# Delta rule pipeline: products of a chunk over two PSUM banks, both products with the state issued first, and a spacing of its own for each chain

## The chip, the cores and the metric

The kernel runs on one core of one Trainium2 chip. The metric is the device time of one execution in microseconds, the median of the runs shown.

## The reference

Two model blocks follow each other on 512 tokens of width 1024. The change lies in the second, in the gated delta rule, which has 8 heads of width 128. What the reference computes for each chunk of a head (it uses chunks of 64 tokens; the kernel uses 4 chunks of 128, which gives the same result):

```python
t_inv = triangular_solve(eye + lmat, eye)        # lmat: strictly lower, from k k^T, decay, beta
u = t_inv @ v_beta
w = t_inv @ (k_beta * exp(gc))
def step(state, xs):
    q_c, k_c, u_c, w_c, a_c, gl = xs
    v_new = u_c - w_c @ state
    o_c = q_c @ state + a_c @ v_new
    state = state * gl + k_c.T @ v_new
    return state, o_c
```

Around it stand a projection of the input (q, k, v and a gate z per head), a causal convolution with SiLU, an RMS norm of o, the gate, and after all heads two more projections.

## The kernel before

All large products are split into two parts of fp32r each (hi and lo), so a product takes three matmuls per 128 rows of depth: whi with h2h, whi with h2l, wlo with h2h. ScalarE makes whi from a weight tile (`wraw`), GpSimd makes wlo (a subtraction of 128x1024 elements, line 359).

The delta stage works in ten slots, t = 0 to 9. In each slot a main generator (`project` of head t for t < 8, `gates` for t = 8 and 9) issues 32 units of three 512-column matmuls into the tag "mm"; here they are called units 0 to 31. After each unit `weave` lets side generators take a step, each at its own start and spacing counted in units:

- `pairs` of head t-1: score products (ta<-kq, gives NU and Aq on VectorE), the transposes of v, then 15 steps of a small solve on VectorE alone (row, dt, dh), which end in dc and Dk.
- `double` of head t-2, eight steps that build the inverse D of 128x128 from 32x32 blocks. Its products are, in order: N with Dk; PX with dc; NU with Dt (32x32 blocks); dc with P1; transposes of D; NU with Dt6; P16 with D. Between two of them VectorE or ScalarE makes the next operand (PX is one of VectorE's).
- `states` of head t-2, chained behind `double`: for each chunk c the products with the state (S with kq, twice), with D (gives vn, on ScalarE), and of vn with kd and with Aq. VectorE makes Wc and the next S, ScalarE and VectorE make the output O. A last step is a reciprocal square root of 4 columns (rs_v, rs_i, rs_j, rs_t, rs_y) and the scaling of O.
- `outputs` of head t-3: four transposes of O and the gate.
- `keys` of head t: norms of q and k, transposes.

TensorE runs in the order in which the generators issue (`chained(True)`, line 1737). The other engines' orders are made by a scheduler when the kernel is built. All products of a chunk but one go to four quarters of one PSUM tile `pa`; the one with kd goes to `pb`. Both have the tag "sm", which has two buffers of one bank each. The tag "tb" of `double` has one buffer. The three lines of `states` that the prediction speaks of most are 1693 to 1696:

```python
K.mm(pa[:, 0:128], kq[:, 0, c], S, start=True, stop=True)
Wc = dp.tile([128, 128], F32, name="Wc", tag="Wc", bufs=2)
nc.vector.scalar_tensor_tensor(Wc, pa[:, 0:128], egc[:, 1, h, c:c + 1], V[:, c], op0=OP.mult, op1=OP.add)
K.mm(pa[:, 128:256], kq[:, 1, c], S, start=True, stop=True)
```

After the last slot the output of head 7 is transposed and gated (line 1750), the stage's pool is closed, and ya is split into yah and yal for the next projection.

Of the kernel before, what the change touches and what calls it, by code (L numbers as in the profile page):

```python
# [11 lines left out]
AF = mybir.ActivationFunctionType  # L12
OP = mybir.AluOpType
# [14 lines left out]

def weave(main, sides):

    sides = [[g, a, d] for g, a, d in sides]
    for u, _ in enumerate(main):
        for q in sides:
            while q[0] is not None and q[1] <= u:
                if next(q[0], sides) is sides:
                    q[0] = None
                q[1] += q[2]
    for q in sides:
        for _ in q[0] or ():
            pass  # L40


def view(ap, off, dims):
# [196 lines left out]
class Core:  # L240
# [36 lines left out]
    chain = None  # L277
# [541 lines left out]
def body(tc, I, out, es):  # L819
# [413 lines left out]
    with ExitStack() as es2:  # L1233
        K.new_sp(es2, 416)
        hp = es2.enter_context(tc.tile_pool(name="hp2", bufs=1))
        nr = ffn(1, x, LAT, (mod['l1'],), lambda: None, hp, nr)
    block2(K, tc, I, out, x[0], mod['b2'], amod, nr)
    K.close_x()


def block2(K, tc, I, out, x, mod, amod, nr):
    nc, ones, ident = K.nc, K.ones, K.ident
    SEG = ((0, 512),)
    with ExitStack() as es:
# [21 lines left out]
        def bc(v, n=128):  # L1266
            return v[:, :, None].to_broadcast([128, v.shape[1], n])
# [18 lines left out]
        t = [dp.tile([128, 4, 8], F32, name=f"g{k}") for k in range(6)]  # L1286
# [21 lines left out]
        esf, egl = eg[:, 0], eg[:, 1]  # L1308
# [49 lines left out]
        scale = 64 ** -0.5  # L1358
        with ExitStack() as es2:
# [14 lines left out]
            for pr in range(2):  # L1374
                ot, zs, st = [], [], []
                for g, d in enumerate(DIL):
# [7 lines left out]
                    q, k, v = qkv  # L1384
# [9 lines left out]
                    for hh in range(2):  # L1394
# [3 lines left out]
                        if g == 0:  # L1398
                            for b0 in (0, 2):
                                p = K.pt("ta")  # L1400
                                for b in (b0, b0 + 1):
                                    o = (b - b0) * 256
                                    k0 = max(b - 1, 0) * 128
                                    n = 256 if b else 128
                                    nc.tensor.matmul(p[:, o + 256 - n:o + 256], q[rows, b * 128:b * 128 + 128], k[rows, k0:k0 + n],
                                                     start=True, stop=True)
# [99 lines left out]
        def t512(name):  # L1506
            return dp.tile([128, 4, 128], F32, name=name, tag=name, bufs=DBS.get(name, 2))
# [4 lines left out]
        def s4(name):  # L1512
            return sp.tile([128, 4], F32, name=name, tag=name, bufs=4)

        def tr4c(src, tag):
            p = K.pt(tag)
            for c in range(4):
                K.tp(p[:, c * 128:c * 128 + 128], src(c), ident)
            return p
# [4 lines left out]
        def project(h, H_):  # L1524

            H_.kq = dp.tile([128, 2, 4, 128], F32, name="kq", tag="kq", bufs=3)
            H_.vc, H_.za = t512("vc"), t512("za").rearrange("p a b -> p (a b)")
            dst = (H_.kq[:, 1].rearrange("p a b -> p (a b)"), H_.kq[:, 0].rearrange("p a b -> p (a b)"),
                   H_.vc.rearrange("p a b -> p (a b)"))
            for k in range(4):  # L1530
                p = K.pt("mm")
                yield from K.gemm_units(next(W), H, p)
                if k < 3:
                    conv(p, 8 * k + h, dst[k])
                else:
                    nc.scalar.activation(H_.za, p, AF.Silu)
                yield
# [143 lines left out]
        def states(h, H_):  # L1681

            kq, kd, V, D, Aq, bk = H_.kq, H_.kd, H_.V, H_.D, H_.Aq, H_.bk
            O = H_.O = t512("O")
            so = H_.so = s4("so")
            junk2 = dp.tile([128, 128], F32, name="junk2", tag="junk2", bufs=1)
            S = None
            for c in range(4):
                pa = K.pt("sm")
                if S is None:  # L1690
                    Wc = V[:, c]
                else:
                    K.mm(pa[:, 0:128], kq[:, 0, c], S, start=True, stop=True)
                    Wc = dp.tile([128, 128], F32, name="Wc", tag="Wc", bufs=2)
                    nc.vector.scalar_tensor_tensor(Wc, pa[:, 0:128], egc[:, 1, h, c:c + 1], V[:, c], op0=OP.mult, op1=OP.add)
                    K.mm(pa[:, 128:256], kq[:, 1, c], S, start=True, stop=True)
                    nc.scalar.activation(O[:, c], pa[:, 128:256], AF.Copy, scale=egc[:, 0, h, c:c + 1])
                    yield
                K.mm(pa[:, 256:384], D[:, c], Wc, start=True, stop=True)
                vn = dp.tile([128, 128], F32, name="vn", tag="vn", bufs=2)  # L1700
                nc.scalar.activation(vn, pa[:, 256:384], AF.Copy, scale=bk[:, c:c + 1])
                yield
                if c < 3:
                    pb = K.pt("sm")
                    K.mm(pb[:, :128], kd[:, c], vn, start=True, stop=True)
                    Sn = dp.tile([128, 128], F32, name="S", tag="S", bufs=2)
                    if S is None:
                        nc.vector.tensor_copy(Sn, pb[:, :128])
                    else:
                        nc.vector.scalar_tensor_tensor(Sn, S, egl[:, c, h:h + 1], pb[:, :128], op0=OP.mult, op1=OP.add)  # L1710
                K.mm(pa[:, 384:512], Aq[:, c], vn, start=True, stop=True)
                if S is None:
                    nc.vector.tensor_copy(O[:, c], pa[:, 384:512])
                else:
                    nc.vector.tensor_add(O[:, c], O[:, c], pa[:, 384:512])
                nc.scalar.activation(junk2, O[:, c], AF.Square, accum_out=so[:, c:c + 1])
                if c < 3:
                    S = Sn
                yield
            nc.vector.tensor_tensor(so, so, H_.rq2, op=OP.mult)  # L1720
            r = K.rsqrt(so, 4, 1.0 / 128, EPS)
            nc.vector.tensor_tensor(r, r, H_.rq, op=OP.mult)
            nc.vector.tensor_tensor(O, O, bc(r), op=OP.mult)

        def outputs(h, H_):
            p = tr4c(lambda c: H_.O[:, c], "sm")
            nc.vector.scalar_tensor_tensor(ya[:, h], p, K.s('dnorm'), H_.za, op0=OP.mult, op1=OP.mult)
            yield

        def gates(j0):  # L1730
            for j in range(j0, j0 + 4):
                p = K.pt("mm")
                yield from K.gemm_units(next(W), H, p)
                nc.scalar.activation(sga[:, j], p, AF.Sigmoid)
                yield

        K.chained(True)
        hs = [Head() for _ in range(8)]
        for t in range(10):
            sides = []  # L1740
            if 0 <= t - 1 < 8:
                sides.append((pairs(t - 1, hs[t - 1]), 1, 1.5))
            if 0 <= t - 2 < 8:
                sides.append((chain(double(t - 2, hs[t - 2]), states(t - 2, hs[t - 2])), 2, 1.6))
            if 0 <= t - 3 < 8:
                sides.append((outputs(t - 3, hs[t - 3]), 8, 1))
            if t < 8:
                sides.append((keys(t, hs[t]), 18, 6))
            weave(project(t, hs[t]) if t < 8 else gates(4 * t - 32), sides)
        weave((), [(outputs(7, hs[7]), 0, 1)])  # L1750
        K.chained(False)
        dp_es.close()
        with ExitStack() as es2:
# [45 lines left out]
```

## Time and profile before

| | us |
|---|---|
| runs shown | 2565.75, 2567.43, 2574.22 (median 2567.43) |
| profiled execution | 2574.59 |
| its span from the first to the last instruction | 2572.8 |
| of it the delta stage, from its first gemm matmul to the first matmul with yah | 2081.7 to 2467.8, 386 |
| mean granted TensorE clock | 0.975 of full speed |

The profiled execution is one execution. Its stretches are compared with each other below by their place in it; times of four digits before the point are microseconds from the start of its span. In the views, PE is TensorE, PEld its weight loads, DVE VectorE, ACT ScalarE and POOL GpSimd. A row by stretch has its bounds, its length, the busy time of PE, PEld, DVE, ACT and POOL (each with the number of instructions), the granted clock as a share of full speed (PEclk), the share of the DMA engines and GB/s.

### The profile page before, as it was taken

The page shows a single profiled execution, that of the slowest core. Times are in us where ns is not written, and L with a number is a line of the kernel's source. Part 1 is how long each engine was busy: PE and PEld are TensorE (multiplying, and loading weights), DVE is VectorE, ACT ScalarE, POOL GpSimd, SP SyncE. Part 2 cuts the span into 40 slices and gives each one's busy share as a digit, 9 for nine tenths or more (in the row PEclk, how much of TensorE's full clock was granted, in tenths as well). Part 3 has the DMA queues.
Part 4 walks back from the last instruction along what each step waited for, and adds up shares of the span by engine and source line. Part 5 has one row for each costly group of instructions (what it writes and reads, how often), then busy time and mean ns, then how long its engine had stood idle before and what let it go on. Part 6 is the DMA issues. An engine that isn't in the chain of part 4 may idle for free.

```text
span 2572.8 us, 33401 instructions
## 1 busy us (share of the span) xinstructions
PE 2415.1 (94%) x12768; PEld 1989.5 (77%) x12768; DVE 1452.3 (56%) x3192; ACT 995.4 (39%) x1952; POOL 697.5 (27%) x318
## 2 busy tenths in 40 slices
PE   8899888999999999989989999999999999998987
PEld 4788777877888888867878788887777787676766
DVE  5957789787475352366785523335331247677454
ACT  4334343232132222334663323333444345555332
POOL 1221111222322223220012344443233342222232
PEclk9999999999999999999999999999999999999999
DMA  7311214425454232121012122233111231111121
GB/s 266 112 49 66 86 57 146 142 79 179 134 168 148 87 116 70 62 93 44 18 50 92 70 101 98 86 111 137 52 63 62 80 117 58 54 58 55 61 99 66
DMA packets 65888, 237.69 MB, mean 92 GB/s; under 512 B 7584, under 2 KB 10560, under 8 KB 50752
## 3 DMA queue, kind: packets, MB, share of 16 engines
q1 hardware_dynamic: 62848, 229.61, 26.2%
q10 hardware_dynamic: 2880, 5.95, 0.7%
q8 instruction: 101, 1.65, 0.3%
q14 instruction: 59, 0.48, 0.1%
HBM read 229.22 MB, written 6.31 MB: 92 GB/s over the span
## 4 chain that ended last, share of the span: by engine, by line
PE 71%; DVE 15%; ACT 4%; issue 3%; DMA 2%; DVEq 0%; ACTq 0%
PE mm L369 13%; PE mm L370 12%; PE mm L372 12%; PE mm L292 6%; PE mm L1190 4%; PE mm L1191 4%; PE mm L1192 4%; DVE ada_acc L421 2%; DMA adaraw<-in_ada_dram 2%; PE tb L292 1%; DVE rs_t L343 1%; PE lv L983 1%; PE sm L292 1%; DVE cv L1347 1%; ACT whi L357 1%
## 5 line engine op out<-in xcount | busy, mean ns | idle before, releaser
L359 POOL TENSOR_TENSOR wlo<-wraw,whi 128x1024 fp32r<-128x1024 f32 (+2 forms) x301 | 682.4, 2269 | 1696.5 <-ACT whi L357 1531.7
L357 ACT ACTIVATE whi<-wraw 128x1024 fp32r<-128x1024 f32 (+2 forms) x301 | 299.6, 996 | 798.3 <-PE mm L370 328.1
L369 PE MATMUL mm<-fhi,whi 128*128 128x512 f32 (+1 forms) x1056 | 374.0, 357 | 1.9 <-ACT fhi L507 1.9
L370 PE MATMUL mm<-flo,whi 128*128 128x512 f32 (+1 forms) x1056 | 359.7, 356 | 0.0
L372 PE MATMUL mm<-fhi,wlo 128*128 128x512 f32 (+1 forms) x1056 | 320.8, 357 | 0.0
L369 PEld LDWEIGHTS mm<-fhi,whi 128*128 128x128 f32 x1056 | 199.0, 189 | 48.4 <-ACT fhi L507 2.7
L370 PEld LDWEIGHTS mm<-flo,whi 128*128 128x128 f32 x1056 | 199.6, 189 | 30.0 <-DVE flo L508 0.2
L421 DVE SCALAR_TENSOR_TENSOR ada_acc<-adaraw,silu_c,ada_acc 128x512 f32<-128x512 f32 x182 | 178.5, 981 | 35.8 <-DMA adaraw<-in_ada_dram 33.7
L372 PEld LDWEIGHTS mm<-fhi,wlo 128*128 128x128 f32 x1056 | 177.5, 191 | 15.0
L1191 PE MATMUL mm<-ffl,whi 128*128 128x512 f32 (+1 forms) x528 | 187.9, 357 | 0.0
L1190 PE MATMUL mm<-ffh,whi 128*128 128x512 f32 (+1 forms) x528 | 186.7, 356 | 1.1 <-ACT ffh L387 1.1
L1192 PE MATMUL mm<-ffh,wlo 128*128 128x512 f32 (+1 forms) x528 | 186.2, 354 | 0.0
L369 PE MATMUL mm<-hhi,whi 128*128 128x512 f32 (+1 forms) x488 | 173.5, 359 | 5.2 <-ACT F L940 3.3
L370 PE MATMUL mm<-hlo,whi 128*128 128x512 f32 x488 | 164.6, 356 | 0.7 <-DVE hlo L508 0.7
L1165 DVE SCALAR_TENSOR_TENSOR fft<-mm,sv,fft 128x511 f32<-128x511 f32 x66 | 43.5, 658 | 187.4 <-ACT fft L1164 187.3
L292 PE MATMUL mm<-h2h,whi 128*128 128x512 f32 x320 | 145.0, 453 | 0.9 <-DVE yb L1491 0.9
L372 PE MATMUL mm<-hhi,wlo 128*128 128x512 f32 (+1 forms) x488 | 143.0, 360 | 0.0
L1194 DVE SCALAR_TENSOR_TENSOR x<-mm,mod_l,x 128x512 f32<-128x512 f32 x64 | 48.0, 750 | 161.5 <-PE mm L1192 161.5
L292 PE MATMUL mm<-h2h,wlo 128*128 128x512 f32 x320 | 128.0, 400 | 0.0
L292 PE MATMUL mm<-h2l,whi 128*128 128x512 f32 x320 | 127.3, 398 | 0.0
L369 PEld LDWEIGHTS mm<-hhi,whi 128*128 128x128 f32 x488 | 95.6, 197 | 27.7 <-ACT F L940 4.3
L1190 PEld LDWEIGHTS mm<-ffh,whi 128*128 128x128 f32 x528 | 99.3, 189 | 16.7 <-ACT ffh L387 1.6
(566 smaller groups left out, 5032.5 us busy)
## 6 DMA issues: line engine op xcount, KB each, us to landing
adaraw<-in_ada_dram SPq DMA_DIRECT2D x208, 256.0 KB, 3.0
wraw<-in_w_up_dram SPq DMA_DIRECT2D x44, 1024.0 KB, 4.7
wraw<-in_w_b_dram SPq DMA_DIRECT2D x40, 1024.0 KB, 4.8
wraw<-in_w_ev_dram SPq DMA_DIRECT2D x14, 1024.0 KB, 4.8
wraw<-in_w_dn_dram SPq DMA_DIRECT2D x16, 768.0 KB, 4.3
wraw<-in_w_dn_dram SPq DMA_DIRECT2D x16, 640.0 KB, 3.8
adaraw<-in_ada_dram SPq DMA_DIRECT2D x16, 512.0 KB, 10.2
wraw<-in_w_evo_dram SPq DMA_DIRECT2D x4, 1024.0 KB, 4.8
```

Of the source, the lines that this page charges most:

```text
L292: return self._link(self.nc.tensor.matmul(*a, **k))
L357: nc.scalar.activation(hi, raw[:, g], AF.Copy)
L359: nc.gpsimd.tensor_sub(lo, raw[:, g], hi.bitcast(F32))
L369: self.nc.tensor.matmul(p, whi[:, k, :], hhi[:, k, c0:c0 + n], start=k == 0, stop=False)
L370: self.nc.tensor.matmul(p, whi[:, k, :], hlo[:, k, c0:c0 + n], start=False, stop=False)
L372: self.nc.tensor.matmul(p, wlo[:, k, :], hhi[:, k, c0:c0 + n], start=False, stop=k == KT - 1)
L421: nc.vector.scalar_tensor_tensor(acc, raw, c[:, kk:kk + 1], acc, op0=OP.mult, op1=OP.add)
L1165: nc.vector.scalar_tensor_tensor(tv[:, 1:], p[:, :n - 1], cw[:, j:j + 1], tv[:, 1:], op0=OP.mult, op1=OP.add)
L1190: nc.tensor.matmul(p, whi[:, k, :], fhi[:, c:c + n], start=k == 0, stop=False)
L1191: nc.tensor.matmul(p, whi[:, k, :], flo[:, c:c + n], start=False, stop=False)
L1192: nc.tensor.matmul(p, wlo[:, k, :], fhi[:, c:c + n], start=False, stop=k == gn - 1)
L1194: nc.vector.scalar_tensor_tensor(xx[:, j], p, m[:, 40 + j:41 + j], xx[:, j], op0=OP.mult, op1=OP.add)
```

## The change

It does four things. The second product with the state is issued right behind the first, ahead of Wc, and both stay in `pa`; the product with D and the two of vn go to a second tile `pb`, so that each tile is one bank with two or three products in it. `weave` takes a list of units for each side generator in place of a start and a spacing; the list gives the unit of each step, and what is left of a generator is issued at the end of the slot. `double` and `states` get lists of their own and stand ahead of `pairs` among the sides. In the last slot both lists are shorter spaced, and `outputs` of head 7 is a side step after unit 31 in place of a call after the slots.

```diff
 def weave(main, sides):
-    sides = [[g, a, d] for g, a, d in sides]
+    sides = [[g, list(us)] for g, us in sides]
     for u, _ in enumerate(main):
         for q in sides:
-            while q[0] is not None and q[1] <= u:
-                if next(q[0], sides) is sides:
-                    q[0] = None
-                q[1] += q[2]
+            while q[1] and q[1][0] <= u:
+                q[1].pop(0)
+                next(q[0], None)
...
+def evenly(a, d, n):
+    return [a + d * k for k in range(n)]
...
             for c in range(4):
-                pa = K.pt("sm")
                 if S is None:
                     Wc = V[:, c]
                 else:
+                    pa = K.pt("sm")
                     K.mm(pa[:, 0:128], kq[:, 0, c], S, start=True, stop=True)
+                    K.mm(pa[:, 128:256], kq[:, 1, c], S, start=True, stop=True)
                     Wc = dp.tile([128, 128], F32, name="Wc", tag="Wc", bufs=2)
                     nc.vector.scalar_tensor_tensor(Wc, pa[:, 0:128], egc[:, 1, h, c:c + 1], V[:, c], op0=OP.mult, op1=OP.add)
-                    K.mm(pa[:, 128:256], kq[:, 1, c], S, start=True, stop=True)
                     nc.scalar.activation(O[:, c], pa[:, 128:256], AF.Copy, scale=egc[:, 0, h, c:c + 1])
                     yield
-                K.mm(pa[:, 256:384], D[:, c], Wc, start=True, stop=True)
+                pb = K.pt("sm")
+                K.mm(pb[:, 0:128], D[:, c], Wc, start=True, stop=True)
                 vn = dp.tile([128, 128], F32, name="vn", tag="vn", bufs=2)
-                nc.scalar.activation(vn, pa[:, 256:384], AF.Copy, scale=bk[:, c:c + 1])
+                nc.scalar.activation(vn, pb[:, 0:128], AF.Copy, scale=bk[:, c:c + 1])
                 yield
                 if c < 3:
-                    pb = K.pt("sm")
-                    K.mm(pb[:, :128], kd[:, c], vn, start=True, stop=True)
+                    K.mm(pb[:, 128:256], kd[:, c], vn, start=True, stop=True)
+                K.mm(pb[:, 256:384], Aq[:, c], vn, start=True, stop=True)
...
-            sides = []
+            sides, last = [], t == 9
+            if 0 <= t - 2 < 8:
+                sides.append((double(t - 2, hs[t - 2]), (0, 2, 3.5, 4.5, 5.5, 6.5, 7.5) if last else (0, 3, 5, 6.5, 8, 9.5, 11)))
+                sides.append((states(t - 2, hs[t - 2]), evenly(9, 1.2, 12) if last else evenly(12.5, 1.7, 11)))
             if 0 <= t - 1 < 8:
-                sides.append((pairs(t - 1, hs[t - 1]), 1, 1.5))
-            if 0 <= t - 2 < 8:
-                sides.append((chain(double(t - 2, hs[t - 2]), states(t - 2, hs[t - 2])), 2, 1.6))
+                sides.append((pairs(t - 1, hs[t - 1]), evenly(1, 1.5, 19)))
             if 0 <= t - 3 < 8:
-                sides.append((outputs(t - 3, hs[t - 3]), 8, 1))
+                sides.append((outputs(t - 3, hs[t - 3]), (8,)))
+            if last:
+                sides.append((outputs(7, hs[7]), (31,)))
             if t < 8:
-                sides.append((keys(t, hs[t]), 18, 6))
+                sides.append((keys(t, hs[t]), (18, 24)))
             weave(project(t, hs[t]) if t < 8 else gates(4 * t - 32), sides)
-        weave((), [(outputs(7, hs[7]), 0, 1)])
```

On VectorE at the start of slot t=5 the order before is this (NU and Aq are made from the score products, O by the end of the reciprocal square root, dc and Dt by `double`):

```order
L342 TENSOR_TENSOR rs_t<-rs_y 128x4
L343 SCALAR_TENSOR_TENSOR rs_t<-rs_t,rs_v 128x4
L345 SCALAR_TENSOR_TENSOR rs_y<-rs_t,rs_y 128x4
L1722 TENSOR_TENSOR rs_y<-rs_y,rq 128x4
L1588 SCALAR_TENSOR_TENSOR NU<-ta,nbk,E 128x128
L1723 TENSOR_TENSOR O<-O,rs_y 128x512
L1588 SCALAR_TENSOR_TENSOR NU<-ta,nbk,E 128x128
L1590 TENSOR_TENSOR Aq<-ta,E 128x256
L1635 TENSOR_TENSOR PX<-tb,dk 128x512
```

And of the changed kernel at the same place:

```order
L1719 TENSOR_TENSOR O<-O,sm 128x128
L1638 TENSOR_TENSOR PX<-tb,dk 128x512
L1724 TENSOR_TENSOR so<-so,rq_17738 128x4
L337 TENSOR_SCALAR rs_v<-so 128x4
L339 TENSOR_SCALAR rs_i<-rs_v 128x4
L341 TENSOR_SCALAR rs_j<-rs_i 128x4
L345 TENSOR_TENSOR rs_t<-rs_j 128x4
L346 SCALAR_TENSOR_TENSOR rs_t<-rs_t,rs_v 128x4
L1591 SCALAR_TENSOR_TENSOR NU<-ta,nbk,E 128x128
```

PX has moved from behind the whole reciprocal square root, both NU and Aq to the place right behind the last O of the slot before, which is ahead of them all.

On VectorE in slot t=5 from the first chunk's S on, before (cv are steps of the convolution, dt and dh of the small solve):

```order
L1708 COPY S<-sm 128x128
L1347 SCALAR_TENSOR_TENSOR cv<-mm,sv,cv 128x511
L1713 COPY O<-sm 128x128
L1347 SCALAR_TENSOR_TENSOR cv<-mm,sv,cv 128x510
L1695 SCALAR_TENSOR_TENSOR Wc<-sm,egc,V 128x128
L1347 SCALAR_TENSOR_TENSOR cv<-mm,sv,cv 128x509
L1619 TENSOR_TENSOR dh<-dh,dt 128x4x2
```

And of the changed kernel:

```order
L1717 COPY O<-sm 128x128
L1621 TENSOR_TENSOR dt<-row,dh 128x24
L1622 TENSOR_TENSOR dh<-dh,dt 128x4x6
L1619 STREAM_SHUFFLE row<-n_18842 128x8
L1621 TENSOR_TENSOR dt<-row,dh 128x20
L1622 TENSOR_TENSOR dh<-dh,dt 128x4x5
L1699 SCALAR_TENSOR_TENSOR Wc<-sm,egc,V 128x128
L1350 SCALAR_TENSOR_TENSOR cv<-mm,sv,cv 128x511
L1621 TENSOR_TENSOR dt<-row,dh 128x16
L1619 STREAM_SHUFFLE row<-n_18842 128x4
L1350 SCALAR_TENSOR_TENSOR cv<-mm,sv,cv 128x510
L1622 TENSOR_TENSOR dh<-dh,dt 128x4x4
```

S and O have moved ahead, to where the small solve still has six of its steps to go; two of these now stand between O and Wc, and one more dh between the convolution's steps.

On ScalarE in slot t=5 before, from the blocks P1 on (N are blocks for the next head, whi is the weights' upper part, cv the convolution's first step, D are blocks of the inverse):

```order
L1504 ACTIVATE N_16821<-nk 32x4x32 x4
L1504 ACTIVATE P_18875<-tb 32x128 x2
L1504 ACTIVATE D_16820<-dc 32x4x32
L357 ACTIVATE whi<-wraw 128x1024
L1344 ACTIVATE cv<-mm,sv 128x512
L1504 ACTIVATE D_16820<-tb 32x4x32 x2
L1504 ACTIVATE Dt_18934<-tb 64x256
```

And of the changed kernel, up to the first chunk's vn and on to the second cv:

```order
L1507 ACTIVATE P_18859<-tb 32x128 x2
L1507 ACTIVATE N_16821<-nk 32x4x32 x4
L1347 ACTIVATE cv<-mm,sv 128x512
L1507 ACTIVATE D_16820<-tb 32x4x32 x2
L360 ACTIVATE whi<-wraw 128x1024
L1507 ACTIVATE Dt_18920<-tb 64x256
L1507 ACTIVATE P_18944<-tb 64x256
L1351 ACTIVATE kq<-cv 128x512
L1705 ACTIVATE vn<-sm,bk 128x128
L1549 ACT_TABLE_LOAD
L1549 ACTIVATE E<-E 128x512
L1347 ACTIVATE cv<-mm,sv 128x512
```

Here whi has moved behind the copies of D, P1 ahead of N, and vn ahead of the table load and E, which stood ahead of it before. In slot t=2 the changed kernel keeps whi ahead of cv, and E ahead of vn.

## Rows read from the trace of the kernel before

**Rows 1.** Stretches of the slots t=3, t=4 and t=5

```profile
2172.66:2217.50 44.84, 41.53 (x223) 31.79 (x222) 29.47 (x137) 24.19 (x68) 9.47 (x4) 0.89 0.15 53
2217.50:2259.58 42.08, 38.77 (x224) 29.92 (x222) 29.40 (x137) 24.20 (x68) 9.50 (x4) 0.96 0.17 57
2259.58:2300.21 40.63, 37.31 (x223) 29.00 (x222) 29.32 (x137) 24.22 (x68) 9.52 (x4) 1.00 0.18 59
```

**Rows 2.** Who TensorE waited for from 2081 to 2468: total, times, longest

```profile
PE sm L292 <- DVE Wc L1695: 17.2, 24, 2.5
PE tb L292 <- DVE PX L1635: 7.9, 7, 1.4
PE sm L295 <- DVE O L1723: 5.8, 1, 5.8
...
PE tb L295 <- ACT D L1504: 1.2, 2, 1.0
```

**Rows 3.** Timeline of TensorE in slot t=5: start, duration, what, idle before

```profile
2262.50 0.97 PE L292 MATMUL tb<-Dk,N 128*128 128x32 f32 x8
...
2265.42 0.39 PE L292 MATMUL mm<-h2h,wlo 128*128 128x512 f32 x1
2266.91 1.08 PE L292 MATMUL tb<-dc,PX 128*128 128x32 f32 x8 [1.10 <-DVE PX L1635]
...
2289.98 0.39 PE L292 MATMUL sm<-S,kq 128*128 128x128 f32 x2
2290.81 0.49 PE L292 MATMUL sm<-S,kq 128*128 128x128 f32 x2 [0.45 <-DVE Wc L1695]
2291.05 0.48 PE L292 MATMUL mm<-h2h,whi 128*128 128x512 f32 x1
...
2292.77 0.60 PE L295 MATMUL ta<-cst,kq 128*128 128x128 f32 x4
2293.13 0.49 PE L292 MATMUL mm<-h2h,whi 128*128 128x512 f32 x1
```

**Rows 4.** Timeline of VectorE and GpSimd in slots t=5 and t=7

```profile
2260.85 2.37 DVE L343 SCALAR_TENSOR_TENSOR rs_t<-rs_t,rs_v 128x4 f32<-128x4 f32 x1
...
2266.17 0.68 DVE L1635 TENSOR_TENSOR PX<-tb,dk 128x512 f32<-128x512 f32 x1
...
2274.11 0.75 DVE L1347 SCALAR_TENSOR_TENSOR cv<-mm,sv,cv 128x511 f32<-128x511 f32 x1 [1.64 <-ACT cv L1344]
...
2363.61 2.38 POOL L359 TENSOR_TENSOR wlo<-wraw,whi 128x1024 fp32r<-128x1024 f32 x1 [6.51 <-ACT whi L357]
2363.80 2.22 DVE L1619 TENSOR_TENSOR dh<-dh,dt 128x8 f32<-128x8 f32 x1
```

**Rows 5.** Timeline of ScalarE in slot t=5, and its table loads by line

```profile
2272.30 1.06 ACT L357 ACTIVATE whi<-wraw 128x1024 fp32r<-128x1024 f32 x1
2273.39 0.69 ACT L1344 ACTIVATE cv<-mm,sv 128x512 f32<-128x512 f32 x1
...
2273.97 0.53 ACT L1504 ACTIVATE D<-tb 32x128 f32<-32x128 f32 x2
...
2274.71 0.41 PE L295 MATMUL tb<-cst,D 64*64 64x64 f32 x4
...
L1546 ACT ACT_TABLE_LOAD x7 | 9.0, 1283 | 5.3 <-DVE E L1545 5.2
```

**Rows 6.** Timeline of TensorE at the end of slot t=9

```profile
2458.97 0.40 PE L292 MATMUL mm<-h2h,wlo 128*128 128x512 f32 x1
...
2465.16 1.12 PE L295 MATMUL sm<-cst,O 128*128 128x128 f32 x4 [5.79 <-DVE O L1723]
...
2467.84 1.65 PE L369 MATMUL mm<-yah,whi 128*128 128x512 f32 x3 [1.57 <-ACT yah L387]
```

**Rows 7.** Busy time and granted clock (PEclk) of two stretches, columns as in rows 1

```profile
2182.00:2192.00 10.00, 10.00 (x54) 6.90 (x53) 5.64 (x31) 4.82 (x14) 2.37 (x1) 0.50 0.12 30
2462.00:2472.00 10.00, 5.27 (x14) 4.00 (x15) 7.73 (x18) 4.27 (x8) 0.96 (x2) 0.50 0.40 140
```

More of the change, by code (lines that the diff above doesn't have):

```diff
@@ L29, in weave @@
 def weave(main, sides):
-    sides = [[g, a, d] for g, a, d in sides]
+    sides = [[g, list(us)] for g, us in sides]
     for u, _ in enumerate(main):
         for q in sides:
-            while q[0] is not None and q[1] <= u:
-                if next(q[0], sides) is sides:
-                    q[0] = None
-                q[1] += q[2]
+            while q[1] and q[1][0] <= u:
+                q[1].pop(0)
+                next(q[0], None)
     for q in sides:
-        for _ in q[0] or ():
+        for _ in q[0]:
             pass
+def evenly(a, d, n):
+    return [a + d * k for k in range(n)]
 def view(ap, off, dims):
@@ L1702, in states @@
                 yield
                 if c < 3:
-                    pb = K.pt("sm")
-                    K.mm(pb[:, :128], kd[:, c], vn, start=True, stop=True)
+                    K.mm(pb[:, 128:256], kd[:, c], vn, start=True, stop=True)
+                K.mm(pb[:, 256:384], Aq[:, c], vn, start=True, stop=True)
+                if c < 3:
                     Sn = dp.tile([128, 128], F32, name="S", tag="S", bufs=2)
                     if S is None:
-                        nc.vector.tensor_copy(Sn, pb[:, :128])
+                        nc.vector.tensor_copy(Sn, pb[:, 128:256])
@@ L1709, in states @@
                     else:
-                        nc.vector.scalar_tensor_tensor(Sn, S, egl[:, c, h:h + 1], pb[:, :128], op0=OP.mult, op1=OP.add)
-                K.mm(pa[:, 384:512], Aq[:, c], vn, start=True, stop=True)
+                        nc.vector.scalar_tensor_tensor(Sn, S, egl[:, c, h:h + 1], pb[:, 128:256], op0=OP.mult, op1=OP.add)
                 if S is None:
-                    nc.vector.tensor_copy(O[:, c], pa[:, 384:512])
+                    nc.vector.tensor_copy(O[:, c], pb[:, 256:384])
@@ L1714, in states @@
                 else:
-                    nc.vector.tensor_add(O[:, c], O[:, c], pa[:, 384:512])
+                    nc.vector.tensor_add(O[:, c], O[:, c], pb[:, 256:384])
                 nc.scalar.activation(junk2, O[:, c], AF.Square, accum_out=so[:, c:c + 1])
```

## The prediction

> **What bounds the kernel now.** I read the views in this order: the stage by slots, who TensorE (PE) waited for in it, the timeline around each kind of wait, the stage's end, and the granted clock. Only the delta stage is touched. An ordinary slot, t=5, takes 40.63 us; VectorE (DVE) is busy for 29.3 of them and ScalarE (ACT) for 24.2 [rows 1], so neither is full and TensorE should set the pace. It is held in three places [rows 2]: 24 times by Wc (17.2 us), 7 times by PX (7.9), and once at the end by O (5.8). Outside these the matmuls follow each other without a gap.
>
> A wait row counts from a modelled end; what TensorE loses is seen between starts. In t=5's second chunk the pair of products with S takes from 2289.98 to the next unit at 2291.05, 1.07 us, with the wait for Wc between the two. Four 128-column matmuls that wait for nothing take 2292.77 to 2293.13, 0.36 [rows 3]. The loss is 0.71, where the row says 0.45. Over all 24 I add 0.29 each: **24.2 us**. By chunk: about 0.7 for the later ones, 1.66 for the first chunk of t=2 to 6, 2.8 in t=7 (longest wait 2.5, [rows 2]). For PX: 2265.42 to 2266.91 is 1.49; the step of one gemm matmul (a third of a unit, 0.24) is in it, so 1.25 is lost [rows 3]; with 0.15 added to each of the seven, **9.0 us**.
>
> **The change, part by part.**
>
> *Both products first, two banks.* The second product with S no longer stands behind DVE's read of the first: TensorE issues four passes and goes on, and the wait for Wc moves to the product with D, one or two units later. Two units with one such product between them take 1.72 (2291.05 to 2292.77, [rows 3]), so a unit is about 0.78; from the pair's start to the product with D there are 0.36 and one unit (1.1 us, third chunk) or two (1.9). Before, Wc was through 0.83 after the pair's start (2290.81); DVE now waits for both products, 0.2 more: 1.05. Gain: the full 24.2, unless Wc itself is late on DVE; that is the third item below.
>
> *Spacing of the double chain.* The order shows PX right behind the last O of the slot before, no longer behind the rsqrt chain, one member of which was held 2.37 us [rows 4]. N·Dk now goes at unit 0 and PX·dc at unit 3: three units and a score product, 3.7 us. The chain between needs 0.97 for N·Dk [rows 3] and 0.68 for PX [rows 4], 1.8 with the hand-overs. So the wait goes in t=3 to 8. In t=9 PX still stands behind that rsqrt member, and 1.4 of it stay: gain 9.0 − 1.4 = **7.6**.
>
> The next step loses a unit of cover: dc·P1 at unit 7, the transposes of D at 8 (before: 7 and 9). Between them ACT must do cv (0.69, steps 0.58) and two copies of D (0.53), 1.1 us from the end of unit 7, and before the change they ended at 2274.50, 0.2 before TensorE needed them [rows 5]. Now TensorE arrives about 1.2 after unit 7, so about 0.2 is lost in t=3 to 7. In t=2 ACT has whi (1.06) ahead of cv: 0.8 more than the 0.2 lost there before. In t=8 a table load (1.28) stands there: 1.05, but that slot lost 0.95 before as well [rows 2, 5]. In t=9 a whi and a Sigmoid stand ahead of the next copy, P16: 1.05. Sum of the double chain's new waits: 0.8 + 5×0.2 + 0.1 + 1.05 = **3.0**.
>
> *Spacing of the states chain, and GpSimd.* This is where I expect new loss. While a wlo of GpSimd runs (2.38 us), a DVE operation on two SBUF tiles stands still: dh of t=7 took 2.22, to the end of the wlo that began at 2363.61, and the rs_t above took 2.37 likewise. The convolution step of 2274.11, which reads PSUM, took 0.75 as always beside the wlo of the whi of 2272.30 [rows 4, 5]. Before, in t=2 to 6, DVE stood in convolution steps when the wlo of the first chunk ran, and was not hit. The order now has dt and dh operations between S and Wc (t=2 to 7), and one dh between the convolution steps behind Wc.
> - t=3 to 6: ACT does vn, then a table load (1.28), E, cv (0.69), a short square, whi (1.06), so the wlo starts over 4 us after vn; by then Wc is past. But the dh behind Wc meets the wlo some 0.5 after its start and is held for the rest, 1.8. Behind it stand two convolution steps, six small operations and then S, on which the next chunk waits; without the hold S would just be in time. I take **1.8 each, 7.2**.
> - t=2 and 7: ACT has whi straight behind vn; the wlo starts between O and the last of those dh, so Wc is late by most of a wlo, as in t=7 before (2.8). I take 1.9 each, **3.8**.
> - t=8, 9: no such operation between S and Wc: 0.3 for a late copy of D in t=8.
>
> The Trainium skill's page "SBUF — State Buffer" (section "SBUF: two separate sides") says that the second read port is one lock between VectorE and GpSimd, and that an operation with two SBUF inputs waits for the whole GpSimd instruction. The trace agrees (2.22 and 2.37 against 2.38). If nothing were held, the sum below would be 11 us better; by the rule it stands.
>
> Bounds of all these: nothing, if no operation meets a wlo and ACT keeps up; or twice as much, 2.38 at each meeting plus ACT's lateness passed on to the next chunk. I take the values above because each is nearest to a hold that the trace has (t=7).
>
> *Last slot.* From the last gemm matmul's step (2458.97 + 0.24) to the first matmul with yah at 2467.84 is 8.6 us; of it the stretch from the transposes' start took 2.68 with the transposes at half clock (1.12); at full they take 0.60 [rows 3], so 2.2 [rows 6]. Now the states end near unit 21 and the transposes follow unit 31 at once, so the rsqrt chain lies beside nine units of gemm: gain **6.4**. The last slot's states chain has one unit between most steps, 1.1 us for the 1.05 above; I take no loss beyond the 1.4 and 1.05 already counted.
>
> *Clock.* In the last rows the clock was granted at half from 2462 to 2472, from some 2.5 us into the idle stretch on [rows 7]. With 1.7 us idle instead of 8 I expect a shorter fall or none: between 0 and 1.9 gained on the ten matmuls to 2472; I take **1.0**.
>
> **Sum.** Removed 24.2 + 7.6 + 6.4 + 1.0 = 39.2; new 3.0 + 7.2 + 3.8 + 0.3 = 14.3; net 24.9. The profiled execution took 2574.59, 7.2 over the median of the runs shown; two falls of the clock in t=3 and 4 cost it about 5.6 (t=3: 44.84 against 40.63, [rows 1, 7]), which explains most of that. I don't expect them in a median, so the sum is set against 2567.43: **2542.5 us**.
>
> **Rivals.**
> 1. *Nothing is held.* DVE and ACT run ahead of my order by half a microsecond and each meeting with a wlo falls beside it. For it: the meetings hang on offsets of 0.5 us. Against it: the wlo is 2.38 long, and the shorter the slot, the less slack DVE has. Gain 39.2 less about 3: 2531.
> 2. *DVE paces the slots.* Holds are passed on from chunk to chunk and double: new waits 29, gain 10, 2557. For it: 29.3 busy of 40.6 leaves 7 us in a 36 us slot, and it works in order. Against: only four wlo run per slot.
> 3. *The first two parts do nothing in t=2 to 8*: the wait for Wc comes back whole at the product with D, the wait for PX at the copies of D; then only the kernel's last slot gains, 6.4: 2561. Against: most losses on Wc were 0.7, and the cover is 1.1 to 1.9 where 1.05 is needed.
> 4. *Slower, through the clock.* In t=3 the clock stood at half for 10 us after a wait for PX of the usual size, and the slot grew by 4.2 [rows 1, 7]. If each of t=2 to 9 had one such fall, 33.6 would outweigh 24.9: 2576. It decides from six slots on. Against: five other waits for PX and the 2.5 of t=7 were not followed by such a fall. The Trainium skill's page "TensorE: Matmul & The Clock Gate" (Part 1) has the clock fall when the array idles; shorter idling, as here, speaks against more falls.
>
> **How the numbers follow.** Forecast 0.52, rival 1 0.20, rival 2 0.16, rival 3 0.08, rival 4 0.04. A measurement of this kernel can't tell changes under about 0.3% (7.7 us; the runs shown spread over 8.5) from none. Faster by more: the first three cases, 0.88; within: rival 3, 0.08; slower: 0.04. The range takes in the forecast, rivals 1 and 2: 2530 to 2558.
>
> **What would show it.** Right: no wait of the second product with S; PX done before its product in t=3 to 8; slots t=3 to 6 near 38.2; dh of 1.5 us or more behind Wc there and a wait of the product with S for S (1 to 2 us); first yah matmul about 2.2 after the last transposes begin. Wrong: slots near 36.4 (rival 1) or 40 (rivals 2, 3), or half clock in several slots (rival 4).

## The result, and the profile after

The changed kernel takes 2542.81 us (median of four, 2541.96 to 2544.83) against 2568.8 for the kernel before (four, 2565.75 to 2574.22): 26.0 us less, a ratio of 0.9898 with an interval of 0.9879 to 0.9916, or 21.6 to 31.1 us. The forecast was 2542.5. In a second, later measurement of the same kernel two executions took 2535.82 and 2541.7 (below).

The profiled execution took 2542.37, its span is 2540.6. The delta stage runs from 2076.84 to 2436.35, 359.5 us against 386.1. The first gemm matmul of the stage comes 4.9 us earlier than before, with the same order of instructions up to there; it is not counted to the change (last section).

Stretches of the changed kernel, columns as in [rows 1]: the slots t=3, 4, 5 and 9, and a part of t=9.

```profile
2167.23:2204.76 37.53, 36.10 (x224) 29.01 (x222) 29.99 (x138) 24.09 (x67) 9.55 (x4) 1.00 0.19 64
2204.76:2242.33 37.57, 36.15 (x223) 29.01 (x222) 29.94 (x138) 24.08 (x67) 9.54 (x4) 1.00 0.19 63
2242.33:2279.88 37.55, 36.12 (x224) 29.01 (x222) 29.97 (x138) 24.08 (x67) 9.54 (x4) 1.00 0.19 65
...
2392.71:2436.35 43.64, 40.92 (x207) 30.91 (x206) 16.00 (x47) 15.45 (x39) 10.55 (x5) 0.80 0.15 49
2398.60:2415.60 17.00, 17.00 (x81) 11.70 (x80) 2.06 (x5) 4.81 (x13) 2.37 (x1) 0.50 0.17 58
```

An ordinary slot takes 37.55 where [rows 1] had 40.63 at full clock, 3.1 less. The last slot does not follow: 43.64, of which 17 us at half clock.

Who TensorE waited for in the stage, as in [rows 2]:

```profile
PE sm L295 <- DVE S L1715: 5.7, 4, 1.4
PE sm L295 <- DVE Wc L1699: 3.0, 2, 1.7
...
PE tb L298 <- ACT D L1507: 1.8, 2, 1.0
...
PE tb L295 <- DVE PX L1638: 1.2, 1, 1.2
...
PE sm L295 <- DVE D L1681: 0.6, 1, 0.6
```

The 24 waits for Wc have become two, the seven for PX one, the 5.8 for O is gone. A row for S is new, four times.

Timeline of slot t=4 in the changed kernel: TensorE, VectorE and GpSimd around the third chunk's products with S.

```profile
2226.15 0.62 PE L295 MATMUL sm<-S,kq 128*128 128x128 f32 x4
...
2230.98 0.39 PE L295 MATMUL mm<-h2h,wlo 128*128 128x512 f32 x1
2232.79 0.71 PE L295 MATMUL sm<-S,kq 128*128 128x128 f32 x4 [1.42 <-DVE S L1715]
...
2227.95 0.74 DVE L1350 SCALAR_TENSOR_TENSOR cv<-mm,sv,cv 128x510 f32<-128x510 f32 x1
2228.60 1.85 DVE L1622 TENSOR_TENSOR dh<-dh,dt 128x16 f32<-128x16 f32 x1
2230.37 0.73 DVE L1350 SCALAR_TENSOR_TENSOR cv<-mm,sv,cv 128x509 f32<-128x509 f32 x1
...
2232.39 0.34 DVE L1715 SCALAR_TENSOR_TENSOR S<-S,eg,sm 128x128 f32<-128x128 f32 x1
...
2228.02 2.40 POOL L362 TENSOR_TENSOR wlo<-wraw,whi 128x1024 fp32r<-128x1024 f32 x1 [7.06 <-ACT whi L360]
```

The four passes with S now stand in one row, with no wait between the two products ([rows 3] had Wc there). Of the wlo that began at 2228.02, dh catches 1.85 where it takes 0.17 alone; the convolution's step ahead of it, which reads PSUM, takes 0.74 beside the same wlo. S ends behind that row of operations, and TensorE's start lies 1.81 behind the one before instead of 0.23: 1.58 lost.

TensorE at the wait for PX in t=9 and at the stage's end (compare [rows 3, 6]):

```profile
2395.45 0.40 PE L295 MATMUL mm<-h2h,wlo 128*128 128x512 f32 x1
2397.01 1.08 PE L295 MATMUL tb<-dc,PX 128*128 128x32 f32 x8 [1.16 <-DVE PX L1638]
...
2433.95 0.39 PE L295 MATMUL mm<-h2h,wlo 128*128 128x512 f32 x1
2434.18 0.60 PE L298 MATMUL sm<-cst,O 128*128 128x128 f32 x4
2436.35 0.96 PE L372 MATMUL mm<-yah,whi 128*128 128x512 f32 x3 [1.57 <-ACT yah L390]
```

From the last gemm matmul's step, 2434.18, to the first matmul with yah there are 2.17 us, before 8.6.

### The profile page after: what moved, and what is told of

Read it like the earlier page. It is cut to its first block, busy times and chain, and to the rows that moved or that the text cites. A ratio compares the mean times of both kernels' runs of the same rounds, so it can differ in the third digit from the quotient of the medians.

```text
span 2540.6 us, 33401 instructions
## 1 busy us (share of the span) xinstructions
PE 2403.3 (95%) x12768; PEld 1986.4 (78%) x12768; DVE 1456.9 (57%) x3192; ACT 994.7 (39%) x1952; POOL 698.4 (27%) x318
## 4 chain that ended last, share of the span: by engine, by line
PE 73%; DVE 13%; ACT 3%; issue 3%; DMA 2%; POOL 0%; DVEq 0%; ACTq 0%
PE mm L372 13%; PE mm L373 13%; PE mm L375 12%; PE mm L295 7%; PE mm L1194 4%; PE mm L1193 4%; PE mm L1195 4%; DVE ada_acc L424 2%; DMA adaraw<-in_ada_dram 2%; PE tb L295 1%; PE lv L986 1%; DVE dh L1622 1%; PE sm L295 1%; PE mm L383 1%; PE mm L384 1%
```

## The experiments

The kernel before was measured again beside each group of runs, and each ratio is to that median: 2570.11 us for the runs with one part alone and the first two on the last slot; 2573.73 for the second profile of the changed kernel, the quarters and the two runs with the small solve closer; 2572.11 for the rest. A comparison of times across these groups is therefore uncertain by up to 5 us. Slots and waits come from one profiled execution of each kernel.

### One part alone: the products, or the spacing

The kernel before with the body of `states` of the changed one:

```diff
                     K.mm(pa[:, 0:128], kq[:, 0, c], S, start=True, stop=True)
+                    K.mm(pa[:, 128:256], kq[:, 1, c], S, start=True, stop=True)
...
-                    K.mm(pa[:, 128:256], kq[:, 1, c], S, start=True, stop=True)
...
-                K.mm(pa[:, 256:384], D[:, c], Wc, start=True, stop=True)
+                pb = K.pt("sm")
+                K.mm(pb[:, 0:128], D[:, c], Wc, start=True, stop=True)
```

> Only the new body of the states chain (both products with S first, two tiles of one bank), with the spacing, the order of the sides and the last slot of before. Theory A (most of the gain is the 24 waits of the second product for Wc, and one step of cover is enough for Wc): those 24 are gone, the 7 waits for PX and the 5.8 us for O at the end stay; 2568.8 less 24 plus about 3 for Wc held by a wlo here and there, 2548 (2543 to 2553). Theory B (the wait only moves to the product with D, the spacing is what carries the gain): 24 waits for Wc at the product with D, 2560 or more.

2555.83 us, ratio 0.9944 (0.9927 to 0.9962), between A and B. Its waits:

```profile
PE sm L295 <- DVE O L1724: 5.8, 1, 5.8
PE sm L292 <- DVE Wc L1696: 3.8, 5, 2.4
PE sm L292 <- DVE S L1710: 3.7, 3, 3.2
PE tb L292 <- DVE PX L1635: 2.8, 7, 1.4
```

The second product with S no longer waits for Wc, and at the product with D Wc is waited for 5 times, so the wait did not move whole to that product, as B had it. A was wrong on PX: its waits did not stay but fell from 7.9 to 2.8 with the spacing of before (0.24 each in t=3 to 8), while ScalarE's P1 is now late by 0.4 in six slots. A also left out other losses: in t=2, S of the first chunk stands behind a dc held 2.42 by a wlo and TensorE waits 3.18; in t=7 Wc is late by 2.36; and six stretches of half clock lie in t=2 to 9. The slots t=4 and 5, which have none, take 38.33, so the products alone give 2.3 of the 3.1 us that a slot gains.

The other half: the changed kernel with the body of `states` of before.

```diff
-                    K.mm(pa[:, 128:256], kq[:, 1, c], S, start=True, stop=True)
                     Wc = dp.tile([128, 128], F32, name="Wc", tag="Wc", bufs=2)
...
+                    K.mm(pa[:, 128:256], kq[:, 1, c], S, start=True, stop=True)
...
-                pb = K.pt("sm")
-                K.mm(pb[:, 0:128], D[:, c], Wc, start=True, stop=True)
+                K.mm(pa[:, 256:384], D[:, c], Wc, start=True, stop=True)
```

> Only the new spacing, the new order of the sides and the shortened last slot, with the body of the states chain of before. Theory A: the waits for PX (7.6) and the end (6.4) are gained; the 24 waits for Wc come back, in part longer than before because a dh held by a wlo now stands ahead of Wc, and the last slot's fall of the clock (about 7 us) stays: 2568.8 less 14.0 plus 7 plus 1 to 6, 2565 (2560 to 2570). Theory B: 2552 or less.

2564.94, ratio 0.9987 (0.9975 to 0.9999): A's number. Waits:

```profile
PE sm L295 <- DVE Wc L1698: 19.7, 24, 3.6
PE tb L298 <- ACT D L1507: 8.6, 7, 2.3
...
PE tb L295 <- DVE PX L1638: 1.2, 1, 1.2
```

All 24 waits for Wc are back and PX is waited for once. A slot t=3 to 6 takes 40.4, only 0.2 less than before. The half clock that A put into the last slot is not there (38.9 us), so A's number was met in part by luck. In its place D is late seven times: with this body whi stands ahead of the convolution's step and of the copies of D on ScalarE, as before the change. The medians' two gains, 14.3 and 5.2, leave 6.5 of 26.0 to the two parts together, and an ordinary slot shows the same: 2.3 and 0.2 of 3.1, with 0.6 left. The split of the medians is rough, since the stretches of half clock differ: some 24 us of them in t=2 to 9 of the run with the products, 10 with the spacing, 17 and 3 in the two profiles of the changed kernel.

### The last slot and its clock

The last slot as every other one:

```diff
-            sides, last = [], t == 9
+            sides, last = [], False
...
+        weave((), [(outputs(7, hs[7]), ())])
         K.chained(False)
```

> The changed kernel with the last slot spaced as every other one and the output of head 7 behind the slots again. Of the last slot the changed kernel's trace shows 6.4 us gained at the end and 17 us of half clock from 1.6 us after the wait for PX on, which cost about 8. Theory A (the fall follows the wait for PX two units behind its first product): here dc with PX comes a unit later, the wait shrinks from 1.2 to about 0.5, the fall in the slot goes, and the end's idle 5.8 us come back with the short fall of before: 2542.8 plus 6.4 plus 1.9 less 8.9, 2542 (2540 to 2545). Theory B (the fall has nothing to do with the last slot's spacing): the fall stays, 2551.

2546.2, ratio 0.9905 (0.9891 to 0.9919). Its last slot, to the first matmul with yah, and two of the waits:

```profile
2393.57:2437.33 43.76, 34.74 (x208) 26.71 (x206) 16.27 (x47) 15.42 (x39) 12.04 (x6) 0.96 0.14 50
```

```profile
PE sm L298 <- DVE O L1727: 5.8, 1, 5.8
...
PE tb L295 <- DVE PX L1638: 0.5, 1, 0.5
```

The slot is as long as that of the changed kernel's first profile, 43.64: what the short spacing saves at the end, the half clock took back in that execution. A's picture of the slot is right; the time is 1 us above its range.

Or with more room ahead of PX:

```diff
-                sides.append((double(t - 2, hs[t - 2]), (0, 2, 3.5, 4.5, 5.5, 6.5, 7.5) if last else (0, 3, 5, 6.5, 8, 9.5, 11)))
-                sides.append((states(t - 2, hs[t - 2]), evenly(9, 1.2, 12) if last else evenly(12.5, 1.7, 11)))
+                sides.append((double(t - 2, hs[t - 2]), (0, 4, 5, 6, 7, 8, 9) if last else (0, 3, 5, 6.5, 8, 9.5, 11)))
+                sides.append((states(t - 2, hs[t - 2]), evenly(10.2, 1.15, 12) if last else evenly(12.5, 1.7, 11)))
```

> The changed kernel, in whose last slot dc with PX comes at unit 4 instead of 2; the other steps follow one unit apart, the states chain from unit 10.2 on. Theory A (the wait for PX in the last slot brings the fall of the clock behind it): the wait of 1.3 us and the 17 us at half clock behind it are gone, 2542.8 less 1.3 less 7 to 9, 2534 (2532 to 2536). Theory B (the fall comes from the many small products of the slot, or stands there by chance): only the wait goes, 2541.5. A new wait of Wc or D in the tighter chain would cost up to 2 us in either.

2540.12, ratio 0.9886 (0.987 to 0.9902). PX is not waited for. VectorE does PX first and dc and Dt only behind the rest of the rsqrt chain, so the wait is now for Dt (timeline), and half clock follows again, for 6.8 us (stretch):

```profile
2399.83 1.64 PE L295 MATMUL tb<-Dt,NU 32*32 32x32 f32 x16 [0.96 <-DVE Dt L1646]
```

```profile
2402.20:2409.00 6.80, 6.80 (x40) 4.73 (x40) 0.16 (x1) 3.03 (x7) 2.35 (x1) 0.50 0.13 18
```

That is near B's time, for a reason that neither theory had. Whether the half clock belongs to the wait was asked of the changed kernel itself, with no edit, in a second profile:

> The changed kernel as it is, for a second profile. In the first its last slot ran 17 us at half clock behind the wait for PX, 43.6 us long; three other kernels with the same wait (only the spacing, one tile for a chunk, second product behind Wc) had no half clock there. If it belongs to this kernel: half clock at the same place again, slot of 42 to 44. If it is chance: a slot near 35, and a time some 8 us lower.

2535.82 and 2541.7. The last slot of this profile and its half clock:

```profile
2391.43:2429.83 38.40, 35.29 (x208) 27.06 (x206) 16.04 (x47) 15.46 (x39) 10.56 (x5) 0.96 0.16 56
2396.70:2400.10 3.40, 3.40 (x13) 2.23 (x13) 1.41 (x6) 1.23 (x4) 0.00 (x0) 0.50 0.00 0
```

The same instructions with the same wait for PX (1.2) bring 3.4 us of half clock here and 17.0 there; the slots t=3 to 8 agree within 0.03. So the length of such a fall is not fixed by the kernel. 13.6 us more of it made the slot 5.24 longer, 0.39 for each us; the 17 us cost about 6.5.

### What holds S: the size of wlo, and the order behind Wc

```diff
-                nc.gpsimd.tensor_sub(lo, raw[:, g], hi.bitcast(F32))
+                for s in (slice(0, 4), slice(4, 8)) if name == 'w_b2' else (slice(0, KT),):
+                    nc.gpsimd.tensor_sub(lo[:, s], raw[:, g, s], hi[:, s].bitcast(F32))
```

> The changed kernel with wlo made in two instructions of 128x512 in place of one of 128x1024, for the weights of the delta stage alone; VectorE's order is the same row for row. Theory A (S and Wc are late because a dt or dh in front of them stands still until the wlo's instruction ends): each hold ends with the first half, some 1.2 us sooner. The four waits for S (1.4 each, 1.5 to 1.6 lost) shrink to 0.3 or less, the waits for Wc of t=2 and 7 (1.3 and 1.7) to about 0.4, that for PX in the last slot (1.2) to nothing: 4x1.2 + 2x1.2 + 1.2 = 8.4 gained, 2534.4; and the half clock behind that wait, 8.9 us, goes or shrinks: 2526 to 2534. Theory C (GpSimd takes the lock again at once for its second half): holds of 1.8 to 2.4 stay, 2543 or a little more. Theory D (VectorE's load of work makes S late, the hold only stands where the time would go anyway): the waits for S stay at 1 us or more with short holds, 2541 to 2543.

2525.97, ratio 0.9813 (0.9796 to 0.9831): the lower end of A's range, though the waits shrank less than A had it. Timeline of VectorE behind Wc of t=4, TensorE's wait there, and two operations in t=7; then the slots t=4 and 9:

```profile
2221.85 0.74 DVE L1623 TENSOR_TENSOR dh<-dh,dt 128x16 f32<-128x16 f32 x1
2222.51 0.74 DVE L1351 SCALAR_TENSOR_TENSOR cv<-mm,sv,cv 128x509 f32<-128x509 f32 x1
2223.17 0.66 DVE L1622 TENSOR_TENSOR dt<-row,dh 128x12 f32<-128x12 f32 x1
...
2225.44 0.71 PE L295 MATMUL sm<-S,kq 128*128 128x128 f32 x4 [0.83 <-DVE S L1716]
...
2330.26 1.26 DVE L1623 TENSOR_TENSOR dh<-dh,dt 128x16 f32<-128x16 f32 x1
2331.56 1.19 DVE L1622 TENSOR_TENSOR dt<-row,dh 128x12 f32<-128x12 f32 x1
```

```profile
2198.04:2234.95 36.91, 36.08 (x223) 29.04 (x222) 29.45 (x138) 24.09 (x67) 10.12 (x8) 1.00 0.19 65
2383.30:2419.14 35.84, 33.83 (x208) 26.18 (x206) 15.34 (x47) 15.46 (x39) 11.11 (x9) 1.00 0.18 59
```

The hold of dh ends with the first half, so C is out. But a second operation meets the second half: 0.57 and 0.50 over their own length in t=4, 1.1 and 1.0 in t=7. That is why the wait for Wc stays in t=7 (1.63) and that for S shrinks to 0.83 and not to 0.3. The wait for Wc in t=2 stays too (1.39). In the last slot rs_t is held 1.29 in place of 2.38, PX comes in time, and no half clock lies in the whole stage: 346.3 us, against 359.5 and, in the changed kernel's second profile, 352.9.

The time fell by more than these waits, because the edit does more than was meant. Its 80 blocks of weights are split from some 1780 us on, ahead of the delta stage, and the stage begins 4 us earlier (2072.8 for 2076.8). The waits for one tile there, of the changed kernel, and of the runs with halves and with quarters (below):

```profile
PE tb L1356 <- DVE dcx L1483: 6.4, 4, 2.8
```

```profile
PE tb L1357 <- DVE dcx L1484: 5.0, 4, 1.7
```

```profile
PE tb L1357 <- DVE dcx L1484: 4.2, 4, 1.5
```

So of the 17 us against the changed kernel's median some 4 lie ahead of the stage, 6.6 are those between 352.9 and 346.3, and the rest is about the 6.6 by which the changed kernel's two profiled stages differ, most of it half clock. That the time reached the lower end of A's range is thus in part luck: 4 us are gained in a place that A left out.

Four pieces instead of two (`slice(k, k + 2) for k in (0, 2, 4, 6)`):

> As the run with halves, with four pieces of 128x256 instead. Theory A (a hold lasts to the end of the piece that is running): the dh of t=3 to 6, held 0.74 with halves, is free after 0.5 or less, the waits for S of 0.83 become 0.4 or less, the slots 36.5; the two operations in front of Wc in t=2 and 7 meet up to three pieces, so the waits of 1.4 and 1.6 fall by at most 0.6: 2526 less 2 to 3, 2523.5. Rival (every operation in the row meets a piece of its own, or GpSimd's pieces cost more in sum): 2526 or more.

2521.45, ratio 0.98 (0.9786 to 0.9813), the fastest version here (the changed kernel measured beside it: 2538.76): a stage of 343.4 us, begun at 2071.8. In t=4:

```profile
2220.08 0.61 DVE L1623 TENSOR_TENSOR dh<-dh,dt 128x12 f32<-128x12 f32 x1
2220.72 0.65 DVE L1622 TENSOR_TENSOR dt<-row,dh 128x8 f32<-128x8 f32 x1
...
2222.57 0.71 PE L295 MATMUL sm<-S,kq 128*128 128x128 f32 x4 [0.70 <-DVE S L1716]
```

A had the waits for S at 0.4 or less; they are 0.70, since two operations are held here as well. Most of the further gain lies in t=2 (38.71 to 37.54) and t=7 (37.91 to 37.30), where the waits for Wc fell to 0.41 and 1.00; a slot t=3 to 6 gains 0.1. The three sizes together give what A needs. Time above the operations' own length between Wc and S: 1.68 (whole), 1.07 (halves), 0.92 (quarters); wait for S: 1.42, 0.83, 0.70. The wait is the hold less about 0.25 each time, so by this estimate S would be just in time with no hold, in this order of VectorE's.

Then the order, with halves and with wlo whole:

```diff
-                sides.append((pairs(t - 1, hs[t - 1]), evenly(1, 1.5, 19)))
+                sides.append((pairs(t - 1, hs[t - 1]), evenly(1, 1.2, 19)))
```

> As the run with halves, and the small solve's steps 1.2 units apart instead of 1.5. By the order this takes the last dt and dh away from between S and Wc and from between the convolution's steps behind Wc in t=3 to 6; a step of the convolution stands ahead of Wc in their place. Theory A: no operation with two inputs in SBUF stands between Wc and the next S when the wlo runs, the waits for S (0.83) go, slots of 36.2, 2526 less 3 to 4, 2522.5. Theory D (VectorE's load makes S late): they stay, 2526; if Wc gets late behind the convolution's step, a wait for Wc of up to 0.6 in each slot, 2525 to 2528.

2533.51, ratio 0.9847 (0.9834 to 0.9861), 11 above A's forecast.

> The spacing of the small solve of the run before this, with wlo whole as in the changed kernel; the orders on VectorE and ScalarE are those of that run. The wlo holds what it meets for up to 2.4 us, but by the order it meets no dh behind Wc. Theory A: the waits for S (1.4, four times) go although the wlo is whole, 2542.8 less 6, 2537 (the wait for PX in the last slot stays, with or without half clock behind it: 2528 without). Theory D: waits for S of 1 us or more stay, 2541 to 2543.

2541.57, ratio 0.9879 (0.9862 to 0.9896): D's number. Of the run with wlo whole, in t=4: TensorE's two waits, VectorE and ScalarE ahead of them; then the slot t=4:

```profile
2218.64 0.41 PE L298 MATMUL tb<-cst,D 64*64 64x64 f32 x4 [0.93 <-ACT D L1507]
2226.17 0.38 PE L295 MATMUL sm<-vn,kd 128*128 128x128 f32 x2
2228.20 0.71 PE L295 MATMUL sm<-S,kq 128*128 128x128 f32 x4 [0.72 <-DVE S L1713]
...
2227.77 0.17 DVE L1622 TENSOR_TENSOR dh<-dh,dt 128x12 f32<-128x12 f32 x1
2227.86 0.28 DVE L1713 COPY S<-sm 128x128 f32<-128x128 f32 x1
...
2216.18 1.26 ACT L1507 ACTIVATE N<-nk 32x128 f32<-32x128 f32 x4 [1.13 <-DVE nk L1611]
```

```profile
2205.04:2242.83 37.79, 36.14 (x223) 28.97 (x222) 28.67 (x138) 24.20 (x67) 9.54 (x4) 1.00 0.19 64
```

The wait for the third chunk's S (line 1715, 1.4 in each of four slots) is gone with wlo whole, as A said, and the size of wlo no longer matters for these slots: 37.8 in both runs. But the wait found another place. The first S (line 1713), which the second chunk's products read, is late by 0.72 in both runs. VectorE has no idle time in the 4.6 us ahead of it: the small solve's steps, now closer to each other, stand in front of S, which begins 1.69 behind the start of its product with kd where the changed kernel has 0.71. So for this S theory D holds. The copies of D are late by 0.93, because ScalarE, whose order up to them is that of the changed kernel, first stands 1.13 for VectorE's nk. That a row of waits is gone is not yet a gain.

### Order or tile: which of the two frees the second product

The order of the change with one tile:

```diff
-                pb = K.pt("sm")
-                K.mm(pb[:, 0:128], D[:, c], Wc, start=True, stop=True)
+                K.mm(pa[:, 256:384], D[:, c], Wc, start=True, stop=True)
...
-                K.mm(pb[:, 256:384], Aq[:, c], vn, start=True, stop=True)
+                K.mm(pa[:, 384:512], Aq[:, c], vn, start=True, stop=True)
```

> The changed kernel with the four products of a chunk in the four quarters of one tile, as before, and only the product with kd in the other; both products with S still come first. Theory A (it is the order of issue that frees TensorE: at the product with D, one or two units later, both readers of the tile are through): 2543, at most 2 off, and slots of 37.6. Theory E (the two banks are what the gain hangs on): the product with D waits for ACT's copy of the second product and the product with Aq for more, 0.3 to 0.7 each 24 times, 2550 to 2560.

Two tiles with the order of before:

```diff
-                    K.mm(pa[:, 128:256], kq[:, 1, c], S, start=True, stop=True)
                     Wc = dp.tile([128, 128], F32, name="Wc", tag="Wc", bufs=2)
...
+                    pb = K.pt("sm")
+                    K.mm(pb[:, 384:512], kq[:, 1, c], S, start=True, stop=True)
```

> The changed kernel with the second product with S behind Wc again, as before, but in the second tile, which DVE does not read for Wc: no bank is shared between that product and Wc. Theory A (before, the wait was for DVE's read of the same tile): the second product does not wait for Wc. It may wait for the tile to come free, whose last reader is the sum into O of the chunk before, right behind S on DVE: 0.3 us or so each, 24 times: 2543 to 2551. Theory F (the second product waits for Wc by the order in which the instructions are written, whatever the tile): 24 waits for Wc of 0.4 and more, 17 us, 2560.

2551.84 (ratio 0.9914, 0.9896 to 0.9932) and 2550.94 (0.9908, 0.989 to 0.9927). One wait of each, of the first and of the second:

```profile
2208.80 0.49 PE L295 MATMUL sm<-Wc,D 128*128 128x128 f32 x2 [0.30 <-ACT O L1700]
```

```profile
2232.08 0.49 PE L295 MATMUL sm<-S,kq 128*128 128x128 f32 x2 [0.36 <-DVE O L1719]
```

By its time the first run fits E, but its waits are not those that E names. With one tile the product with D waits for ScalarE's read, 0.30 in one chunk of each slot t=2 to 7; besides it waits 2.2 and 2.4 in t=2 and 7, where the changed kernel has 1.3 and 1.7 for Wc. With the tiles split and the old order the second product waits 0.16 to 0.37 for the tile's last reader and never for Wc. So either alone removes the 24 waits of the second product for Wc.

The some 9 us by which both are slower than the changed kernel are no price of the tile or of the order. D is late seven times by 0.9 to 2.3, 8.7 and 8.6 us in place of 1.8, since ScalarE's order has whi ahead of the copies of D again, as in the run with the spacing alone; the four waits for S of 1.4 are down to 0.4 or less in both; and half clock stands elsewhere (10 us in t=2, 7 and 8 with one tile, 14 in t=8 with the old order). A slot t=3 to 6, with none, takes 38.3 and 39.0 against 37.55. What order and tile are worth against each other stays open.

The last version has the halves and a longer start of the last slot:

> The halves of the run before last but one and, in the last slot, one unit more between the first two steps of the inverse (units 0, 3, 5, 6, 7, 8, 9, the states chain from 10.2 on). Theory A: the holds shrink as in the run with halves, and in the last slot neither PX nor Dt is waited for, so that no half clock follows: 2542.8 less 8.4 less up to 8.9, 2526 to 2530. If the half clock of the last slot comes without a wait: 2533 to 2535. Theory C or D: 2540.

2529.89, ratio 0.9828 (0.9809 to 0.9847): in A's range, but by the halves alone, which took 2525.97. The edit gained nothing: the last slot takes 36.89 against 35.84, with new waits for Dt (0.5, 0.6), which A had gone, and O (0.3).

## Why the prediction was right

*The waits removed* (24.2 forecast for Wc, 7.6 for PX, 6.4 at the end) came as worked out. No second product with S waits; PX is in time in t=2 to 8, and in t=9 1.3 are left where 1.4 were said; the end takes 2.17 where 2.2 were said.

*The double chain* cost less than the 3.0: the transposes of D are not late in t=3 to 7 (0.2 each was said). In t=2 and 8 the forecast holds (waits of 0.9 and 1.0). In t=9, where 1.05 was said for P16, the first profile has no wait and the second 0.36.

*The holds by wlo* were the step with most doubt, and hold in place and size: dh for 1.85 in t=3 to 6, S late, 1.58 lost each for the 1.8 said; Wc late in t=2 and 7, 1.5 (and 0.4 at S) and 1.85 for the 1.9 said. That the Trainium skill's rule on the shared port decides here (page "SBUF — State Buffer", section "SBUF: two separate sides") the runs with pieces bear out: with the same order on VectorE row for row, a slot fell from 37.55 to 36.9 only because GpSimd's instruction ends sooner.

*Late in t=8*: 0.3 said, 1.1 seen (D behind VectorE's copy 0.8, vn 0.3).

*The clock* is the term that was wrong: 1.0 gained was said. The fall at the stage's end did go, but one came inside the last slot and cost 6.5 in the first profile; in the second profile of the kernel it was 3.4 us long. The sum was right in spite of it: the stage, set against the one before less the 5.6 of its falls in t=3 and 4, is 21.0 shorter in the first profile and 27.6 in the second, around the forecast of 24.9. A slot of 37.55 where 38.2 was said (0.2 of D, 0.2 of S, the rest small) made up for part of the clock. The mechanisms held; that the median came within 0.3 us of the forecast is luck, for the two profiled executions of the kernel are 6.6 apart and the two medians 4.

*The rivals.* DVE as the pace (2557) is out: it is busy for as long in the run with halves (29.45) and the slots are shorter. Nothing held (2531) is out by dh's 1.85. That the first two parts do nothing (2561) is out by the waits. Falls in every slot (2576): there is none in t=2 to 8 of either profile. The argument against them, that shorter idling brings fewer falls, is not borne out by all runs: the kernel with the products alone waits less than the one before (20 us against 32 in t=2 to 9) and has six falls in t=2 to 9, where that one has three.

## What to carry to other kernels

In this kernel a wait for another engine's read of a tile was cut by issuing the second writer first or, as well, by giving it a tile of its own. Then ask what stands between the reader and the next operand on the reader's engine, for that is where the next wait appears. Where GpSimd and VectorE both work from SBUF, the length of one GpSimd instruction is a price that VectorE's small operations on two SBUF tiles pay (0.17 alone, 1.85 beside a wlo): wlo cut in four, with VectorE's order as it was, gave 14.6 us between two profiled executions (9.5 in the stage, of which 1.3 are a stretch of half clock, and 5.1 ahead of it), about half of what the whole change gave. And an edit to one chain moves the scheduler's order on the other engines, so a run of one part alone carries that order's waits too; read them before giving the time to the part.

## What the runs showed of the hardware that was not expected

The half clock of the last slot differs from execution to execution of one kernel, 17.0 and 3.4 us, and another length, 6.8, follows the same wait in the run with wlo whole and the small solve closer. The same wait for PX of 1.2 was followed by none in the last slot in the three runs with the spacing alone, with one tile and with the second product behind Wc. A wait of this size is thus not enough to bring it; what decides its length stays open.

A hold ends with GpSimd's current piece, yet an operation that follows can be held again by the next one: at 2330.26 and 2331.56 two in a row by the two halves.

Ahead of the delta stage nothing differs in the order of TensorE's and ScalarE's instructions between the kernels before and after, and still the stage began between 2075.9 and 2081.7 in the ten profiles with wlo whole. (In the four with wlo in pieces it began between 2070.9 and 2072.8, earlier than in any of the ten, so there a gain ahead of the stage is shown, but not its exact size.) So for the change itself a difference of some us between two profiled executions is read inside the stage, and the 4.9 us by which the stage began earlier are not counted to the change.
